# The h of a feed-forward transposed by VectorE and a round trip through device memory

## The chip, the cores and the metric

One core of a Trainium2 chip runs the whole kernel. The metric is the device time of one execution in microseconds (us). The kernel before takes 1023.84 us, the median of three runs (1023.41 to 1024.4). Engines are named as in the profile: PE is TensorE, DVE is VectorE, ACT is ScalarE, POOL is GpSimd, SP is SyncE, whose queue issues nearly all DMAs.

## The reference

Two layers, each a half-step SwiGLU feed-forward, a token mixer of four head groups and a second half-step SwiGLU, then a final RMS norm. There are 256 tokens, 1024 columns, and 2816 columns inside a feed-forward. The change touches the four feed-forwards alone:

```
def swiglu(x, w_gate, w_up, w_down):
    return (jax.nn.silu(x @ w_gate) * (x @ w_up)) @ w_down

for l in range(DEPTH):
    x = x + 0.5 * swiglu(rms_norm(x, norm_ffn1[l]), ffn1_w_gate[l], ffn1_w_up[l], ffn1_w_down[l])
    x = x + hybrid_mixer(rms_norm(x, norm_mix[l]), ...)
    x = x + 0.5 * swiglu(rms_norm(x, norm_ffn2[l]), ffn2_w_gate[l], ffn2_w_up[l], ffn2_w_down[l])
```

All is float32. The kernel gets there by splitting every factor of a product into a rounded high part and a low part and multiplying three times.

## The kernel before, in words

The tokens are two halves, h = 0 and h = 1, of 128 each. The weights come as *sets* of 128 x 1024 numbers (512 KB) in one list for the whole program. Loading a set (`Set.load`) is a DMA into one of four raw buffers, an ACT instruction that rounds it to `whi`, and a DVE instruction that subtracts to `wlo`; there are eight buffers of these. Using a set (`Set.mm`) is six matmuls of 512 columns: for each of two row blocks `hi x whi`, `hi x wlo`, `lo x whi`.

A feed-forward has 11 chunks of 256 inner columns. A chunk is four sets of gate and up columns (s = 0 to 3, `gate_up`), whose product gathers in one PSUM bank `ps_g`; after s = 3, ACT takes the silu and DVE multiplies, which gives `sg`, 128 tokens x 256 columns, the h of the reference. The product with `w_down` wants it the other way round, columns on partitions. So `turn` waits three turns and lets TensorE transpose two blocks of 128 x 128 into PSUM; ACT and DVE split that into `hhi` and `hlo`. After the gate and up sets of chunk c come the two sets of `w_down` of chunk c - 1 (`down_`), summed in `ps_d0` and `ps_d1` over the 11 chunks.

The loop at the end calls `consume(0, i)` for the set i and `consume(1, i - 5)` for the other half, five sets later (two at the very start). Each `consume` loads two sets ahead, issues the six matmuls and then calls `advance`, which counts down the waits of all spawned generators: a "turn" is one `consume`. On this recorded program lies a scheduler, which puts the instructions of each engine in an order of its own, within their dependences; an engine then runs its list strictly in order. SP too: a DMA that waits for its data or its buffer holds up all DMAs behind it.

Of the kernel before, what the change touches and what calls it, by code (L numbers as in the profile page):

```python
# [9 lines left out]
F32 = mybir.dt.float32  # L10
F32R = mybir.dt.float32r
# [4 lines left out]
P = 128  # L16
# [9 lines left out]
AHEAD = 2  # L26
TURN_X = 1
TURN_H = 3
WARM = 30
FIRST = 12  # L30
FIRST_LAG = 2
# [14 lines left out]
)  # L46
WIDTH = dict(SPLITS)
GW = tuple(sum(WIDTH[n] for n in g) for g in GROUPS)
# Rows of w_out in the order in which the heads are done: NSA, FoX, dilated, sinks.
OROWS = (2, 3, 0, 1, 6, 7, 4, 5)  # L50


# [1 line left out]
def hybrid_kernel(ctx: ExitStack, tc: tile.TileContext, a: dict, out: bass.AP):  # L54
    nc = tc.nc
# [5 lines left out]
    hbuf = pool("hbuf", 2)  # L61
    gains = pool("gains", 1)
    work = pool("work", 2)
    small = pool("small", 4)
    ps = pool("ps", 2, space=PSUM)
    dram = pool("dram", 2, space=bass.MemoryType.DRAM)

    def bank(tag):
        return ps.tile([P, 512], F32, name=f"ps_{tag}")
# [20 lines left out]
            for g in tbl:  # L90
                nc.sync.dma_start(tbl[g], a[f"c_{g}"])

    # The array runs at half its clock until it has been busy for a while.
    idle = const.tile([P, P], mybir.dt.bfloat16, name="idle")
    nc.vector.memset(idle, 0.0)
    one = const.tile([P, 1], F32, name="one")
# [8 lines left out]
        return bass.AP(tensor=src.tensor, offset=src.offset, ap=[[0, P], [1, n]])  # L105

    class Set:
        """Two row blocks of a weight by up to 512 of its columns."""

        def __init__(self, src, n, use):  # L110
            self.src, self.n, self.use = src, n, use
# [39 lines left out]
    running = [[], []]  # L151

    def spawn(gen):
        """Runs gen, which yields how many turns it lets pass."""
        wait = next(gen, None)
        if wait is not None:
            alive.append([gen, wait])

    def queue(h, gen):
        """As spawn, one after the other for each h; one that yields 0 lets the next begin."""  # L160
        lines[h].append(gen)

    def advance():
# [21 lines left out]
        begins.setdefault((i, h), []).append(f)  # L185

    class Norm:
        """RMS norm of x: its product with the gain, transposed, in two parts, for the matrix
        products; the scale of each token goes onto what these return."""

        def __init__(self, src, final=False):
            self.src, self.final = src, final
# [2 lines left out]
            self.parts = {}  # L195

        def load(self, before):
            """Fetches the gain, well before the sets from this one on."""
            self.gain = gains.tile([P, D], F32, name="gain")
            with tc.issue_after(sets[before - 8].dma.ins):  # L200
                nc.sync.dma_start(self.gain, bcast(self.src, D))

        def take(self, h, c):
            """Half c of the columns of x[h] is final."""
            if c == 0:
                self.stat[h] = small.tile([P, 2], F32, name="stat")
            sl = slice(c * 512, (c + 1) * 512)
            xg = work.tile([P, 512], F32, name="xn")
            self.first = nc.vector.tensor_tensor(xg, x[h][:, sl], self.gain[:, sl], op=ALU.mult)
            norm_stat(h, c, self.stat[h])  # L210
            if self.final:
                self.xg[h, c] = xg
            else:
                spawn(self.turn(h, c, xg))
            if c == 1:
                self.scale[h] = rstd_of(self.stat[h])

        def take_turned(self, h, c):
            """As take, of the kernel's input, which is there in both layouts."""
            xg = work.tile([P, 512], F32, name="xn").rearrange("p (k t) -> p k t", t=P)  # L220
            nc.sync.dma_start(xg, a["xT"][h, c])
            g = gcol[:, 4 * c:4 * c + 4].unsqueeze(2).to_broadcast([P, 4, P])
            self.first = nc.vector.tensor_tensor(xg, xg, g, op=ALU.mult)
            hi, lo = (big.tile([P, 4, P], F32R, name=f"x{t}{h}{c}") for t in ("hi", "lo"))
            split_T(xg, hi, lo)
            self.parts[h, c] = hi, lo
# [14 lines left out]
            self.parts[h, c] = hi, lo  # L241

        def blocks(self, h, ks):
            """The stationary operands of some blocks of 128 columns."""
            while any((h, k // 4) not in self.parts for k in ks):
                advance()
            return tuple([self.parts[h, k // 4][t][:, k % 4, :] for k in ks] for t in range(2))
# [6 lines left out]
    def add_ffn(norm, gu, down, nxt):  # L254
        phases.append(len(sets))
        hT = {}
        acc = {}

        def turn(h, c, hh):
            yield TURN_H  # L260
            pt = quad("t")
            for j in range(2):
                nc.tensor.transpose(pt[:, j, :], hh[:, j * P:(j + 1) * P], ident)  # L263
            hT[h, c] = tuple(hbuf.tile([P, 2, P], F32R, name=f"h{t}{h}") for t in ("hi", "lo"))
            split_T(pt[:, :2, :], *hT[h, c])

        def gate_up(h, c, s, st):
            if s == 0:
                acc[h] = bank("g")
            st.mm(acc[h], *norm.blocks(h, (2 * s, 2 * s + 1)), s == 0, s == 3)  # L270
            if s == 3:
                sg = work.tile([P, 256], F32, name="sg")
                r = norm.scale[h]
                nc.scalar.activation(sg, acc[h][:, :256], AF.Silu, scale=r)  # L274
                nc.vector.scalar_tensor_tensor(sg, acc[h][:, 256:], r, sg, op0=ALU.mult, op1=ALU.mult)  # L275
                spawn(turn(h, c, sg))

        def down_(h, c, d, st):
            if c == 0:
                acc[h, d] = bank(f"d{h}")  # L280
            hi, lo = hT[h, c]
            st.mm(acc[h, d], [hi[:, k, :] for k in range(2)], [lo[:, k, :] for k in range(2)], c == 0, c == 10)
            if c == 10:
                residual(h, d, acc[h, d], 0.5, nxt)

        def add_down(c):
            for d in range(2):
                sets.append(Set(down[c, d], 512, lambda h, st, d=d: down_(h, c, d, st)))

        for c in range(11):  # L290
            for s in range(4):
                sets.append(Set(gu[c, s], 512, lambda h, st, c=c, s=s: gate_up(h, c, s, st)))
            if c > 0:
                add_down(c - 1)
        add_down(10)

    def add_mixer(l, norm, nxt):
# [28 lines left out]
                V[name] = big.tile([P, 2, n, 64], F32, name=f"v_{name}")  # L326

        def tr(z, n):
            """Transposes n pieces of 128 columns into one bank."""
            pt = quad("t")  # L330
            for j in range(n):
                nc.tensor.transpose(pt[:, j, :], z[:, j * P:(j + 1) * P], ident)  # L332
            return pt

        def dup(dst, src, n, r):
            """n heads of 64 columns, each twice."""
            scaled(dst.rearrange("p (n t d) -> p n t d", n=n, t=2),
                   src.rearrange("p (n d) -> p n d", n=n).unsqueeze(2).to_broadcast([P, n, 2, 64]), r)

# [4 lines left out]
            nc.scalar.activation(dst, src, AF.Copy, scale=r)  # L344

        def scores(qT, keys, nk, tag):
            """Minus q k^T, for even and for odd heads, in a bank each."""
            views = [bank(tag)[:, :2 * nk].rearrange("p (j k) -> p j k", j=2) for _ in range(2)]
            for i in range(4):
                r = slice(64 * (i % 2), 64 * (i % 2) + 64)  # L350
                dst = views[i % 2][:, i // 2, :]
                nc.tensor.matmul(dst, qT[r, i // 2, :], keys(i)[r, :nk], start=True, stop=True)  # L352
            return views

        def softmax(h, views, table, nk, sink=None, guard=False):
            """exp(least - s) of the negated scores, and one over its sums."""
            p = work.tile([P, 4, P * (h + 1)], F32, name=f"p{h}")[:, :, :nk]
            nm = small.tile([P, 4], F32, name="nm")
            den = small.tile([P, 4], F32, name="den")
# [59 lines left out]
            return put  # L419

        def put_part(h, first, last):
            """Adds up the branches of NSA."""
            def put(o):
                if first:
                    M["on", h] = work.tile([P, 2, P], F32, name="on")
                    nc.scalar.activation(M["on", h], o, AF.Copy)
                else:
                    nc.vector.tensor_tensor(M["on", h], o, M["on", h], op=ALU.add)
                if last:
                    hi, lo = oT[h]  # L430
                    split_T(M["on", h], hi[:, 0:2, :], lo[:, 0:2, :])
                    ready[h].add(0)
            return put
# [46 lines left out]
                              lambda i, n: M["vc"], put_part(h, False, True), NB, f"d{h}", gate=0, guard=True)  # L480

        def log_sigmoid(h, z, r):
            """min(z, 0) - log(1 + exp(-|z|)); the logarithm as 2 artanh(e / (2 + e))."""
            sm = lambda n: small.tile([P, 4], F32, name=n, bufs=2)
            zf = sm("zf")
            nc.vector.scalar_tensor_tensor(zf, z, r, M["fb"], op0=ALU.mult, op1=ALU.add)
# [18 lines left out]
            nc.vector.scalar_tensor_tensor(M["lf", h], q, -2.0, m0, op0=ALU.mult, op1=ALU.add)  # L505

        def forget(h):
            """The sums of log f up to each key, to all partitions, with the causal mask on the
            block of the queries themselves."""
            yield 2  # L510
            pc = bank("t")
            if h == 0:
# [231 lines left out]


def _layout(i):
    """The inputs as the kernel reads them: the same numbers, in another order."""
    f = lambda n: np.asarray(i[n], np.float32) if np.asarray(i[n]).dtype != np.float32 else np.asarray(i[n])
    r = {"x": f("x").reshape(2, P, D)}
    r["xT"] = np.ascontiguousarray(r["x"].reshape(2, P, 2, 4, P).transpose(0, 2, 4, 3, 1))  # L750
# [38 lines left out]
```

## Time and profile before

| | |
|---|---|
| median of three runs | 1023.84 us |
| span of the profiled execution, first to last instruction | 1021.8 us |
| its own time | not listed; the timed median is 2.0 us over the span |
| PE busy | 1007.5 us, 99% of the span |
| PE clock | 0.999 of full speed, on average |
| DMA | 183.53 MB, 179 GB/s over the span |
| wraw loads (512 KB), issue to landing | 3.4 us median |

A busy PE says only that some matmul was under way; two overlap. The distance from one start to the next in the timeline is what a matmul costs. The DMA share is the mean over the 16 DMA engines of the time in which they had a packet in hand.

### The profile page before, as it was taken

The numbers are of one execution on the slowest core, as the hardware profiler recorded it, in microseconds if no ns is written. First come the engines' busy times: TensorE is split into PE (matmuls) and PEld (weight loads), VectorE is DVE, ScalarE is ACT, GpSimd is POOL, SyncE is SP. The second block draws the span as 40 slices with busy tenths as digits, with TensorE's granted clock in tenths as the row PEclk, the third lists the DMA queues.
The fourth block names the chain that finished last, engine by engine and source line by source line (L and its number), as shares of the span: only waits on it lengthen the run. The fifth ranks groups of instructions, "written<-read, shape, count | busy, mean of one in ns | idle before, by whom it ended". The sixth has DMA issues, their size and how long they took to land.

```text
span 1021.8 us, 13721 instructions
## 1 busy us (share of the span) xinstructions
PE 1007.5 (99%) x5046; PEld 814.9 (80%) x5046; DVE 617.5 (60%) x1150; ACT 519.9 (51%) x881; POOL 20.0 (2%) x31
## 2 busy tenths in 40 slices
PE   9999999999999999999999999999999999999996
PEld 6888888867778888888888888888678788888885
DVE  6655555786777455555765555558777665555554
ACT  6544444655665444444544444446566554444442
POOL 0000000010000000000000000000100000000000
PEclk9999999999999999999999999999999999999999
DMA  8955556655344455556656555655634445555551
GB/s 304 304 188 187 186 188 205 189 155 161 119 165 146 162 187 186 185 186 209 186 175 192 185 186 186 211 171 178 200 96 149 133 159 188 193 186 186 185 185 41
DMA packets 56722, 183.53 MB, mean 180 GB/s; under 512 B 7232, under 2 KB 14032, under 8 KB 56656
## 3 DMA queue, kind: packets, MB, share of 16 engines
q1 hardware_dynamic: 55920, 181.09, 54.7%
q0 software_dynamic: 448, 1.06, 0.4%
q8 instruction: 39, 0.64, 0.3%
q10 hardware_dynamic: 288, 0.52, 0.1%
q14 instruction: 27, 0.22, 0.1%
HBM read 181.59 MB, written 1.06 MB: 179 GB/s over the span
## 4 chain that ended last, share of the span: by engine, by line
PE 92%; DVE 5%; ACT 2%; issue 1%; DMA 0%; SPq 0%; POOLq 0%; ACTq 0%
PE ps_g L127 55%; PE ps_d L127 28%; PE ps_t L263 2%; PE ps_t L410 2%; DVE wlo L121 1%; PE ps_t L398 1%; PE ps_d L352 1%; PE ps_t L238 1%; PE ps_t L332 1%; ACT p L369 1%; PE ps_t L352 1%; DVE blk L441 1%; DMA xn<-in_xT 0%; DVE x L251 0%; DVE p L390 0%
## 5 line engine op out<-in xcount | busy, mean ns | idle before, releaser
L121 DVE TENSOR_TENSOR wlo<-wraw,whi 128x1024 fp32r<-128x1024 f32 (+2 forms) x328 | 394.6, 1205 | 285.9 <-ACT whi L119 285.1
L119 ACT ACTIVATE whi<-wraw 128x1024 fp32r<-128x1024 f32 (+2 forms) x328 | 342.2, 1044 | 315.6 <-PE ps_g L127 218.8
L127 PE MATMUL ps_g<-whi,xhi 128*128 128x512 f32 (+2 forms) x896 | 351.0, 392 | 0.6 <-ACT whi L119 0.6
L127 PE MATMUL ps_g<-wlo,xhi 128*128 128x512 f32 (+2 forms) x896 | 347.0, 387 | 0.9 <-DVE wlo L121 0.9
L127 PE MATMUL ps_g<-whi,xlo 128*128 128x512 f32 (+2 forms) x896 | 346.9, 387 | 0.0
L127 PEld LDWEIGHTS ps_g<-whi,xhi 128*128 128x128 f32 x896 | 168.8, 188 | 37.2 <-issue 4.7
L127 PEld LDWEIGHTS ps_g<-wlo,xhi 128*128 128x128 f32 x896 | 168.9, 188 | 32.9 <-DVE wlo L121 1.8
L127 PEld LDWEIGHTS ps_g<-whi,xlo 128*128 128x128 f32 x896 | 168.7, 188 | 31.6 <-issue 0.3
L127 PE MATMUL ps_d<-whi,hhi 128*128 128x512 f32 x352 | 144.2, 410 | 0.5 <-ACT hhi L143 0.5
L127 PE MATMUL ps_d<-whi,hlo 128*128 128x512 f32 x352 | 137.9, 393 | 0.0
L127 PE MATMUL ps_d<-wlo,hhi 128*128 128x512 f32 x352 | 137.5, 391 | 0.0
L127 PEld LDWEIGHTS ps_d<-whi,hlo 128*128 128x128 f32 x352 | 66.1, 188 | 14.4 <-DVE hlo L144 0.2
L274 ACT ACTIVATE sg<-ps_g,rstd 128x256 f32<-128x256 f32 x88 | 41.8, 475 | 69.8 <-PE ps_g L127 67.4
L127 PEld LDWEIGHTS ps_d<-whi,hhi 128*128 128x128 f32 x352 | 66.2, 188 | 12.6 <-ACT hhi L143 1.5
L127 PEld LDWEIGHTS ps_d<-wlo,hhi 128*128 128x128 f32 x352 | 66.4, 189 | 11.5
L275 DVE SCALAR_TENSOR_TENSOR sg<-ps_g,rstd,sg 128x256 f32<-128x256 f32 x88 | 42.4, 481 | 43.3 <-ACT sg L274 43.3
L369 ACT ACTIVATE p<-p,nm 128x128 f32<-128x128 f32 (+2 forms) x96 | 40.1, 421 | 23.1 <-DVE nm L361 10.8
L143 ACT ACTIVATE hhi<-ps_t 128x256 fp32r<-128x256 f32 x88 | 33.0, 375 | 27.2 <-PE ps_t L263 27.2
L144 DVE TENSOR_TENSOR hlo<-ps_t,hhi 128x256 fp32r<-128x256 f32 x88 | 33.8, 417 | 8.5 <-ACT hhi L143 8.5
L263 PEld LDWEIGHTS ps_t<-ident,sg 128*128 128x128 f32 x176 | 24.6, 140 | 11.4
L263 PE MATMUL ps_t<-ident,sg 128*128 128x128 f32 x176 | 33.5, 271 | 0.0
L139 POOL TENSOR_TENSOR rstd<-ms,mhalf 128x1 f32<-128x1 f32 x14 | 8.6, 613 | 940.0 <-DVE ms L137 940.0
(146 smaller groups left out, 593.4 us busy)
## 6 DMA issues: line engine op xcount, KB each, us to landing
wraw<-in_gu SPq DMA_DIRECT2D x176, 512.0 KB, 3.4
wraw<-in_down SPq DMA_DIRECT2D x88, 512.0 KB, 3.4
wraw<-in_win SPq DMA_DIRECT2D x24, 512.0 KB, 4.0
wraw<-in_wout SPq DMA_DIRECT2D x16, 512.0 KB, 3.5
wraw<-in_win SPq DMA_DIRECT2D x16, 384.0 KB, 3.5
wraw<-in_w SPq DMA_DIRECT2D x8, 512.0 KB, 3.4
wraw<-in_win SPq DMA_DIRECT2D x8, 400.0 KB, 3.4
gain<-in_norm_ffn SPq DMA_DIRECT2D x3, 512.0 KB, 4.4
```

The lines of the kernel that those rows point to most:

```text
L119: nc.scalar.activation(self.hi, r, AF.Copy)
L121: nc.vector.tensor_tensor(self.lo, r, self.hi.bitcast(F32), op=ALU.subtract)
L127: nc.tensor.matmul(acc, s, w[:, k, :], start=first and k == 0 and i == 0, stop=last and k == 1 and i == 2)
L143: nc.scalar.activation(hi, pt, AF.Copy)
L144: nc.vector.tensor_tensor(lo, pt, hi.bitcast(F32), op=ALU.subtract)
L238: nc.tensor.transpose(pt[:, j, :], xg[:, j * P:(j + 1) * P], ident)
L263: nc.tensor.transpose(pt[:, j, :], hh[:, j * P:(j + 1) * P], ident)
L274: nc.scalar.activation(sg, acc[h][:, :256], AF.Silu, scale=r)
L275: nc.vector.scalar_tensor_tensor(sg, acc[h][:, 256:], r, sg, op0=ALU.mult, op1=ALU.mult)
L352: nc.tensor.matmul(dst, qT[r, i // 2, :], keys(i)[r, :nk], start=True, stop=True)
L369: nc.scalar.activation(p[:, i, :], p[:, i, :], AF.Exp, bias=nm[:, i:i + 1], scale=-1.0, accum_out=den[:, i:i + 1])
L410: nc.tensor.matmul(o[64 * e:64 * e + 64, j, :], vals(2 * j + e, n), pts[n][:w, 2 * j + e, :], start=n == 0, stop=n == len(blocks) - 1)
```

## The change

The new `turn_far` serves chunks 0 to 9; chunk 10 keeps `turn`. As soon as `sg` is there, DVE transposes each of its 32 x 32 blocks within its place (`st`). The block that belongs at block row b, block column a then still stands at row a, column b. Four DMAs, one for each 32 partitions, write `st` to device memory, 32 partitions x 8 pieces of 128 bytes each. Three turns later one DMA reads it back (`back`, 128 partitions x 2 pieces of 512 bytes), with the blocks in their places, and three turns after that ACT and DVE split it. All five DMAs go through SP's queue. `st` uses the mixer's buffers `z` and `back` its buffers `pT`. `down_` calls `advance` until its h is there. The pool in device memory gets four buffers in place of two. The rest of the diff takes comments out.

```
-    dram = pool("dram", 2, space=bass.MemoryType.DRAM)
+    dram = pool("dram", 4, space=bass.MemoryType.DRAM)
...
+FAR = 3
...
+        def turn_far(h, c, hh):
+            st = work.tile([P, 512], F32, name="z")[:, :256]
+            nc.vector.transpose(st, hh)
+            far = dram.tile([8, 32, 4, 32], F32, name="far")
+            for a_ in range(4):
+                nc.sync.dma_start(far[:, :, a_, :].rearrange("b j i -> j b i"),
+                                  st[32 * a_:32 * a_ + 32].rearrange("p (b i) -> p b i", i=32))
+            yield FAR
+            back = work.tile([P, 4, P], F32, name="pT")[:, :2, :]
+            nc.sync.dma_start(back, far.rearrange("(k b) j a i -> (b j) k (a i)", k=2))
+            yield FAR
+            hT[h, c] = tuple(hbuf.tile([P, 2, P], F32R, name=f"h{t}{h}") for t in ("hi", "lo"))
+            split_T(back, *hT[h, c])
...
-                spawn(turn(h, c, sg))
+                spawn((turn if c == 10 else turn_far)(h, c, sg))
...
+            while (h, c) not in hT:
+                advance()
```

SP's queue of one chunk of the first feed-forward, before (numbers tell buffers apart; `in_gu1` are the gate and up sets, `in_down1` the sets of `w_down`):

```order
L116 DMA wraw_1238<-in_down1 128x1024
L116 DMA wraw_1259<-in_down1 128x1024
L116 DMA wraw_1287<-in_gu1 128x1024
L116 DMA wraw_1312<-in_gu1 128x1024
L116 DMA wraw_1331<-in_gu1 128x1024
L116 DMA wraw_1350<-in_gu1 128x1024
```

The same of the kernel after, where line numbers are higher by one; `far_925` belongs to h = 1, `far_947` to h = 0:

```order
L275 DMA far_925<-z_923 32x8x32 x4
L117 DMA wraw_930<-in_down1 128x1024
L117 DMA wraw_960<-in_gu1 128x1024
L275 DMA far_947<-z_945 32x8x32 x4
L279 DMA pT_958<-far_925 128x2x128
L117 DMA wraw_980<-in_gu1 128x1024
L279 DMA pT_972<-far_947 128x2x128
L117 DMA wraw_1007<-in_gu1 128x1024
L117 DMA wraw_1026<-in_gu1 128x1024
L117 DMA wraw_1044<-in_down1 128x1024
```

Of six DMAs to a chunk there are sixteen now, ten rows here: the writes wait for their transpose on DVE and the reads for the landing of their writes, and the loads stand behind them. In the other feed-forwards the writes stand one load sooner or later; the reads stand before the last gate and up loads of the chunk there too.

ACT in one chunk before (`hhi1` and `hhi0` are split from PSUM, where TensorE wrote them):

```order
L274 ACTIVATE sg_996<-ps_g_934,rstd_274 128x256
L119 ACTIVATE whi_1001<-wraw_999 128x1024
L274 ACTIVATE sg_1011<-ps_g_947,rstd_219 128x256
L119 ACTIVATE whi_1029<-wraw_1027 128x1024
L143 ACTIVATE hhi1_1023<-ps_t_1020 128x256
L143 ACTIVATE hhi0_1042<-ps_t_1039 128x256
L119 ACTIVATE whi_1054<-wraw_1052 128x1024
L119 ACTIVATE whi_1073<-wraw_1071 128x1024
```

and after, where they are split from the read-back tile `pT`:

```order
L291 ACTIVATE sg_942<-ps_g_871,rstd_219 128x256
L120 ACTIVATE whi_932<-wraw_930 128x1024
L120 ACTIVATE whi_962<-wraw_960 128x1024
L291 ACTIVATE sg_1062<-ps_g_996,rstd_274 128x256
L144 ACTIVATE hhi1_992<-pT_958 128x256
L120 ACTIVATE whi_982<-wraw_980 128x1024
L144 ACTIVATE hhi0_1003<-pT_972 128x256
L120 ACTIVATE whi_1009<-wraw_1007 128x1024
L120 ACTIVATE whi_1028<-wraw_1026 128x1024
L120 ACTIVATE whi_1046<-wraw_1044 128x1024
L291 ACTIVATE sg_1084<-ps_g_1013,rstd_219 128x256
```

Both splits now wait for a DMA, with the rounding of the next sets behind them. The silu of h = 1 (`sg_1062`) now comes two sets after that of h = 0 of the same chunk (`sg_942`); before, it stood just ahead of that of the next chunk.

PE around the transposes of h = 0 before (`ps_t<-ident,sg`):

```order
L127 MATMUL ps_d0_391<-whi_980,hhi0_912 128x512
L127 MATMUL ps_d0_391<-wlo_981,hhi0_912 128x512
L127 MATMUL ps_d0_391<-whi_980,hlo0_913 128x512
L263 MATMUL ps_t_1039<-ident_86,sg_1011 128x128 x2
L127 MATMUL ps_d1_472<-whi_871,hhi1_893 128x512
L127 MATMUL ps_d1_472<-wlo_872,hhi1_893 128x512
L127 MATMUL ps_d1_472<-whi_871,hlo1_894 128x512
L127 MATMUL ps_d1_472<-whi_871,hhi1_893 128x512
```

and the last matmuls of the gate and up sets of h = 0 in the kernel after (`ps_g_1013` is h = 0, `ps_g_1138` h = 1; buffers 1009 and 1010 are of the set s = 2, 1028 and 1029 of s = 3):

```order
L128 MATMUL ps_g_1013<-wlo_1010,xhi01_181 128x512
L128 MATMUL ps_g_1013<-whi_1009,xlo01_182 128x512
L128 MATMUL ps_g_1013<-whi_1009,xhi01_181 128x512
L128 MATMUL ps_g_1013<-wlo_1010,xhi01_181 128x512
L128 MATMUL ps_g_1013<-whi_1009,xlo01_182 128x512
L128 MATMUL ps_g_1013<-whi_1028,xhi01_181 128x512
L128 MATMUL ps_g_1138<-whi_982,xhi10_224 128x512
L128 MATMUL ps_g_1013<-wlo_1029,xhi01_181 128x512
L128 MATMUL ps_g_1013<-whi_1028,xlo01_182 128x512
L128 MATMUL ps_g_1013<-whi_1028,xhi01_181 128x512
L128 MATMUL ps_g_1013<-wlo_1029,xhi01_181 128x512
L128 MATMUL ps_g_1013<-whi_1028,xlo01_182 128x512
```

The transposes are gone (8 pairs are left in the program, of chunks 10, where there were 88). Single matmuls of h = 1 now stand between those of h = 0 that wait for `whi` and those that wait for `wlo`, and h = 1 uses a set one to three sets after h = 0, not five.

## Rows read from the trace of the kernel before

**Rows 1.** The page, part 1: busy time, share of the span, instructions of each engine.
```profile
PE 1007.5 (99%) x5046; PEld 814.9 (80%) x5046; DVE 617.5 (60%) x1150; ACT 519.9 (51%) x881; POOL 20.0 (2%) x31
```

**Rows 2.** The page, part 4: the chain that ended last, by engine and line.
```profile
PE 92%; DVE 5%; ACT 2%; issue 1%; DMA 0%; SPq 0%; POOLq 0%; ACTq 0%
PE ps_g L127 55%; PE ps_d L127 28%; PE ps_t L263 2%; PE ps_t L410 2%; DVE wlo L121 1%; PE ps_t L398 1%; PE ps_d L352 1%; PE ps_t L238 1%; PE ps_t L332 1%; ACT p L369 1%; PE ps_t L352 1%; DVE blk L441 1%; DMA xn<-in_xT 0%; DVE x L251 0%; DVE p L390 0%
```

**Rows 3.** The chain in order of time, 410 to 440 us: start, duration, what.
```profile
412.93 10.88 PE ps_g L127 x48
423.81 1.36 PE ps_d L127 x6
425.18 0.22 PE ps_t L263 x2
425.39 1.40 PE ps_d L127 x6
```

**Rows 4.** The timeline of SP's queue (start, us, what): two stretches.
```profile
151.97 0.43 SPq L313 DMA_DIRECT2D fb<-in_fox_b_f  x1
152.44 0.42 SPq L314 DMA_DIRECT2D sinkin<-in_swa_sinks  x1
...
410.78 0.33 SPq L116 DMA_DIRECT2D wraw<-in_down  x1
...
427.61 0.33 SPq L116 DMA_DIRECT2D wraw<-in_down  x1
```

**Rows 5.** The timeline of one h product, same columns, with what ended a wait.
```profile
422.06 0.39 PE L127 MATMUL ps_g<-whi,xlo 128*128 128x512 f32 x1
422.49 0.47 ACT L274 ACTIVATE sg<-ps_g,rstd 128x256 f32<-128x256 f32 x1 [1.66 <-PE ps_g L127]
423.00 0.48 DVE L275 SCALAR_TENSOR_TENSOR sg<-ps_g,rstd,sg 128x256 f32<-128x256 f32 x1 [0.91 <-ACT sg L274]
```

**Rows 6.** Busy time in two stretches: length, engines, clock, DMA share, GB/s.
```profile
0.00:50.00 50.00, 47.46 (x211) 37.33 (x212) 31.64 (x42) 29.63 (x43) 1.52 (x7) 1.00 0.87 304
349.00:467.00 118.00, 118.00 (x535) 97.29 (x534) 62.61 (x72) 54.62 (x70) 0.00 (x0) 1.00 0.58 189
```

**Rows 7.** Groups by line and shape: count, busy us, mean ns, idle before.
```profile
L121 DVE TENSOR_TENSOR wlo<-wraw,whi 128x1024 fp32r<-128x1024 f32 x304 | 371.5, 1224 | 277.1 <-ACT whi L119 276.5
L119 ACT ACTIVATE whi<-wraw 128x1024 fp32r<-128x1024 f32 x304 | 321.9, 1060 | 299.2 <-PE ps_g L127 202.6 <-PE ps_d L127 91.4 <-PE ps_t L263 1.5
L403 DVE COPY pT<-ps_t 128x512 f32<-128x512 f32 x10 | 6.9, 688 | 9.8 <-PE ps_t L398 6.6 <-PE ps_t L410 3.2
L390 DVE TENSOR_SCALAR p<-p,rd 128x256 f32<-128x256 f32 x24 | 6.8, 350 | 0.1
```

**Rows 8.** The DMA view: queue share; issues with KB each, median us to landing.
```profile
q1 hardware_dynamic: 55920, 181.09, 54.7%
wraw<-in_gu SPq DMA_DIRECT2D x176, 512.0 KB, 3.4
out_y<-xn SPq DMA_DIRECT2D x2, 256.0 KB, 2.0
line<-ct POOLq DMA_DIRECT2D x4, 2.0 KB, 3.0
gcol<-in_gcol SPq DMA_DIRECT2D x1, 4.0 KB, 1.7
```

**Rows 9.** The DMA view, 657.8 to 658.2 us: small packets and their busy share.
```profile
DMA packets 237, 0.01 MB, mean 36 GB/s; under 512 B 237, under 2 KB 237, under 8 KB 237
q1 hardware_dynamic: 237, 0.01, 38.3%
```

**Rows 10.** Waits of SP's queue: us in total, times, longest.
```profile
SPq L116 <- DVE wlo L121: 590.4, 235, 12.6
```

**Rows 11.** The DMA view, 42 to 46 us, where other loads share the queue.
```profile
wraw<-in_down SPq DMA_DIRECT2D x1, 512.0 KB, 5.7
```

## The prediction

> **What bounds the kernel now.** Read first the busy shares [rows 1]: PE 99%, its weight loads (PEld, which overlap it) 80%, DVE 60%, ACT 51%. That alone proves little, since matmuls overlap, so the chain that ended last comes next [rows 2]: 92% of the span is PE, and 83% is the two groups of matmuls that use the sets, ps_g and ps_d of line 127. The transposes of h (L263) are 2%. Then the chain in order of time [rows 3] gives prices: 48 matmuls take 10.88 us, 0.2267 each, and the feed-forward's stretch is these without a gap. SP's queue shows the same beat: the first w_down load of one chunk is issued at 410.78 and of the next at 427.61 [rows 4], 16.83 us to a chunk. The 72 matmuls of a chunk (6 sets, 2 halves, 6 each) are 72 x 0.2267 = 16.32 of that. The other 0.51 is two transposing turns. In a long stretch of a feed-forward [rows 6] PE is busy 118.00 of 118 us at a granted clock of 1.00, the higher of the two levels, 2.4 GHz; DVE 62.61, ACT 54.62, DMA share 0.58. SP waits mostly for wlo to free a raw buffer [rows 10]: loads are held back, not hurried. So every slot that leaves PE is time, as long as the sets still come in time.
>
> **What is removed.** A pair of transposes is 0.22 us in the chain, and the six matmuls behind it take 1.40 instead of 1.36 [rows 3]: 0.26, which agrees with the 0.51 for two. Of 88 turns 80 go (10 chunks, 2 halves, 4 feed-forwards): 80 x 0.255 = 20.4 us. ACT and DVE still split h, from SBUF instead of PSUM, which I leave at nothing; both have idle time for it.
>
> The Trainium skill prices the step otherwise: its page "VectorE: DVE Perf Modes", section "The three transpose paths", gives TensorE 390 ns for a 128 x 128 transpose (in bf16), and would have 160 x 0.39 = 62 us go. The row shows 0.22 us for two in a full queue, and it decides.
>
> **What is added, off PE.** A turn adds one DVE transpose of 128 x 256. No row shows one. The nearest are a DVE pass over the same shape, 350 ns, and one over twice the columns, 688 [rows 7]; I take 0.35, so 0.7 us to a chunk beside 62.61 / 118 x 16.83 = 8.9 us of DVE now. It is hidden under PE.
>
> It adds four writes and one read on SP. An issue takes 0.47 us from one to the next [rows 4]: ten more to a chunk, sixteen in all, 7.5 of 16.3 us. No bound.
>
> On the DMA engines a turn adds 4 x 256 packets of 128 bytes, 64 for each of 16 engines, and a read of 128 KB. A set costs 0.58 x 118 us / 42 sets = 1.63 us of the engines, so the read 0.41. The writes are the unknown: no row shows 128 bytes going to device memory. Below: 237 packets under 512 bytes, nearly all reads, took 38.3% of 16 engines for 0.4 us [rows 9], 10 ns each. Above: a packet of the page's mean, mostly 4 KB, takes 0.547 x 1021.8 x 16 / 55920 = 160 ns [rows 8]. I take 18 ns, near the lower row, since these packets are small but not as small: 1.15 us to a turn. The DMA work of a chunk is then 9.8 + 2 x (1.15 + 0.41) = 12.9 of 16.3 us. It fits, but not by much.
>
> The Trainium skill speaks against it: "DMA: Bandwidth & Descriptors", section "Specifications", says that transfers under 512 bytes are read, modified and written. From its 27 GiB/s to an engine, 512 bytes read and written would be some 35 ns a packet, an estimate. No run here shows it yet; by it the DMA work of a chunk would be 15.1 us, and the forecast below would stand.
>
> **What is added on the path: SP's order.** SP was free to run ahead; now the loads stand behind writes that wait for a product of the same chunk, and reads that wait for those writes. So there are two loops from one chunk's writes to the next, and each must be shorter than 16.32 us, or it, not PE, sets the beat. I follow the first feed-forward's order as shown with the change.
>
> Common head, from the last gate matmul of h = 0: a matmul's tail beyond its slot and the hop to ACT 0.20, silu to product 0.51, product 0.48 [rows 5], transpose 0.35, hop 0.10: 1.64 us.
>
> Loop A, through the read for h = 1 and the load of set s = 1 behind it: head 1.64, four write issues 1.88, the read's issue 0.47, the load 3.4 to landing [rows 8] plus 0.41 behind the read, whi 1.06 and wlo 1.23 [rows 7] with a hop of 0.05, and then the 22 matmuls from there to the end of s = 3 (the last 12 are in the order shown), 4.99. Sum 15.1: slack 1.2 us.
>
> Loop B, through the read for h = 0, which waits for its writes: head 1.64, three issues 1.41, the fourth write's landing, the read's issue 0.47, the load of s = 2 3.81, whi, wlo and hop 2.34, 12 matmuls 2.72. A DMA lands at least after 1.7 us (gcol, 4 KB); the writes to device memory took 2.0 (out_y) and 3.0 (line) [rows 8]. With 2.0 the sum is 14.4: slack 1.9, so a landing up to 3.9 us costs nothing.
>
> Both are under 16.32, so PE stays the bound: queued behind the waiting reads are three loads, with over a microsecond to spare, and behind the splits on ACT the rounding of the same sets, which would wait for their loads anyway. With packets at p each, the writes delay loop A by 64p - 2.35 us and land 64p + 0.4 after the last issue; either slack is used up near p = 55 ns. From there each microsecond costs 40 (chunks with round trips).
>
> **The start.** In the first 50 us the DMA share is 0.87 [rows 6], with inputs, tables and the first sets in one queue: 6.5 us free. Seven turns fall into it, 7 x 1.56 = 10.9 us: 4.4 too much, of which I take 4.0. At 10 ns it would be 0.9, at 55 ns 21. After the mixers the weights flow already; I add nothing.
>
> **The sum.** Profiled span 1021.8 - 20.4 + 4.0 = 1005.4; with the 2.0 us by which the median stands above the span, 1007.4. Own range: 1002 to 1016 (start from 0.9 to 11 us, transposes' price by 10%).
>
> **Rivals.**
> - *The small writes set the beat* (slower). Place: the read for h = 0 on SP, waiting for the fourth write. It decides from 55 ns a packet. For it: between 10 and 160 ns nothing is shown, and pieces of 128 bytes in steps of 512 are new to this kernel. Against: the small reads at 10 ns. At 75 ns: 64 x 0.020 = 1.3 us x 40 = 51, so 1059. At the far end, 160 ns, the engines would need 9.8 + 0.8 + 20.5 = 31.1 us to a chunk, 14.8 x 40 = 590 more; I give that next to nothing.
> - *The loads land later, behind the others.* Loop A has 1.2 us to spare for the load's 3.4. Where other loads shared the queue one took 5.7 [rows 11]; at that, 2.3 - 1.2 = 1.1 x 40 = 44, so 1051; at 5.0 it would be 0.4 x 40 = 16, so 1023, which is no change. For it: the loads now leave SP in bunches of three. Against: in loop A only a read of 128 KB is ahead.
> - *The transposes cost PE more than the chain shows*, as the skill's 390 ns would have it: 1007 - 42 = 965. The beat of 16.83 speaks against it.
> - *The change does not take the transposes away*: excluded by the order, where 8 pairs of 88 are left.
>
> **How the numbers follow.** Forecast 0.62; small writes 0.18; later loads 0.17, a third of it with no change or a small gain; dearer transposes 0.02; the rest 0.01. Range 1001 to 1050: it leaves out under 0.05 below and some 0.15 above. About 0.2%, 2 us, is what a measurement of this kernel can tell from no change. Faster takes the forecast, the dearer transposes and a little of the late loads: 0.66; same 0.06; slower 0.28.
>
> **What would show it.** Right: a beat of 16.3 us between first w_down loads, PE's chain at 0.227 us a matmul in the feed-forwards, writes landing under 3.9 us, and the time lost mostly before 60 us. Wrong: PE waiting for whi or wlo at s = 1 or s = 2 of every chunk; SP's reads waiting for far for several us; a DMA share near 1 in the feed-forwards; a granted clock of half where PE pauses. If the beat is over 16.8, the forecast is wrong, whatever the reason.

## The result and the profile after

The kernel after takes 1034.33 us (median of four runs, 1033.16 to 1036.79) against 1024.12 of the kernel before beside it: a ratio of 1.0103, interval 1.0087 to 1.0119. It is slower, by 10 us, where a gain of 16 was forecast (1007.4 from 1023.84). Its profiled execution took 1033.17 us, with a span of 1031.4.

The page, parts 1 and 4, answering to [rows 1, 2]:

```profile
PE 1001.0 (97%) x4886; PEld 800.8 (78%) x4886; DVE 649.6 (63%) x1230; ACT 518.9 (50%) x881; POOL 21.4 (2%) x31
...
PE 77%; DMA 7%; DVE 7%; ACT 4%; issue 2%; SPq 2%; POOLq 0%; POOL 0%; ACTq 0%; DVEq 0%
```

PE lost 160 matmuls and 6.5 us of busy time, yet the span grew: PE's share of the chain fell from 92% to 77%, and DMA, SP and ACT have come into it. What they wait for, in the view of the waits (us in total, times, longest), answers to [rows 10]:

```profile
SPq L275 <- DVE z L272: 208.2, 67, 7.9
SPq L117 <- DVE wlo L122: 206.4, 103, 12.6
...
SPq L279 <- DMA far<-z: 18.8, 19, 3.0
```
```profile
ACT whi L120 <- DMA wraw<-in_gu: 99.7, 84, 3.3
ACT hhi L144 <- DMA pT<-far: 61.1, 29, 4.9
```

SP used to wait 590 us for free buffers, which is a reserve. Of that, 206 is left; as much again goes into writes (L275) that wait for VectorE's transpose, with loads standing behind them. Hence ACT waits 84 times for gate and up loads. In the DMA view the median load takes 4.4 or 6.0 us to landing, against 3.4 in [rows 8]; the median write takes 1.7:

```profile
wraw<-in_gu SPq DMA_DIRECT2D x176, 512.0 KB, 4.4
wraw<-in_down SPq DMA_DIRECT2D x88, 512.0 KB, 6.0
far<-z SPq DMA_DIRECT2D x320, 32.0 KB, 1.7
pT<-far SPq DMA_DIRECT2D x80, 128.0 KB, 3.2
```

**Where the time went.** A feed-forward ends with its fourth `x<-ps_d` on DVE. From the end of the stage ahead of it to there, the four took 199.7, 188.6, 188.5 and 186.9 us before and 209.1, 187.6, 190.6 and 185.4 after; the mixers changed by under half a microsecond. So the first lost 9.4 us, the third 2.1, and the second and fourth won 1.0 and 1.5, where 5 were expected of each.

Three places show it. The first is the start. SP's timeline at 60 to 80 us (start, us, what):

```profile
60.29 4.07 SPq L275 DMA_DIRECT2D far<-z  x8
64.53 0.38 SPq L279 DMA_DIRECT2D pT<-far  x1
64.96 0.47 SPq L117 DMA_DIRECT2D wraw<-in_gu  x1
...
68.33 0.84 SPq L92 DMA_DIRECT2D tbl_cmp<-in_c_cmp  x1
69.34 0.54 SPq L279 DMA_DIRECT2D pT<-far  x1
69.92 2.55 SPq L117 DMA_DIRECT2D wraw<-in_gu  x3
```

and what the chain makes of it, followed by PE in two windows (length, then busy time and count of PE, PEld, DVE, ACT, POOL, the clock, the DMA share, GB/s):

```profile
69.92 6.87 DMA wraw<-in_gu
...
76.87 1.06 ACT whi L120
...
77.96 1.23 DVE wlo L122
```
```profile
70.00:80.00 10.00, 8.08 (x34) 5.84 (x33) 4.54 (x6) 4.52 (x6) 0.00 (x0) 1.00 0.99 358
...
189.00:195.00 6.00, 3.73 (x9) 2.63 (x9) 5.18 (x7) 4.38 (x6) 0.00 (x0) 0.72 0.35 115
```

Between the issue of one gate load at 64.96 and of the next at 69.92 stand seven table loads and a read; then three loads go out together, and the one that PE needs lands 6.87 us later. The first window holds 34 matmuls where ten microseconds hold 44 at 0.227.

The second place is the beat of the first feed-forward. The first of four writes of h = 0 leaves SP at these times, 16.7 and 16.8 us apart, hardly shorter than the 16.83 of [rows 4]:

```profile
119.53 1.81 SPq L275 DMA_DIRECT2D far<-z  x4
...
136.19 1.80 SPq L275 DMA_DIRECT2D far<-z  x4
138.10 0.40 SPq L279 DMA_DIRECT2D pT<-far  x1
138.54 0.47 SPq L117 DMA_DIRECT2D wraw<-in_gu  x1
139.29 0.37 SPq L279 DMA_DIRECT2D pT<-far  x1
139.77 0.87 SPq L117 DMA_DIRECT2D wraw<-in_gu  x2
...
152.96 1.81 SPq L275 DMA_DIRECT2D far<-z  x4
```

The chain there is loop B, term by term:

```profile
139.77 6.18 DMA wraw<-in_gu
...
146.03 1.07 ACT whi L120
...
147.13 1.24 DVE wlo L122
...
148.41 3.01 PE ps_g L128 x12
```

First write to issue of the read 3.10 (139.29 - 136.19), to the load 0.48, landing 6.18, rounding and subtraction 2.46, twelve matmuls 3.01, head 1.54 (152.96 - 151.42): 16.77 us.

The third is the end of the first and of the third feed-forward: the window 189 to 195 us above has nine matmuls in six microseconds, at a clock of 0.72. It is not the landing of a load that PE waits for there. SP issues two loads of `w_down` at 180.65, and the first of them lands 5.0 us after its issue, at 185.6 (SP's timeline, and the DMA view at 180.6 to 180.7 us):

```profile
180.65 0.96 SPq L117 DMA_DIRECT2D wraw<-in_down  x2
```
```profile
wraw<-in_down SPq DMA_DIRECT2D x1, 512.0 KB, 5.0
```

ACT rounds it only at 189.61, because in ACT's list its rounding stands behind a split and the last silu of h = 1, which both wait for PE. The chain there:

```profile
188.50 0.71 PE ps_g L128 x3
...
189.24 0.02 ACT sg L291
...
189.61 1.05 ACT whi L120
...
190.69 1.24 DVE wlo L122
...
191.97 8.23 PE ps_d L128 x29
```

PE waits first for the rounding and then for the subtraction: three starts of matmuls, at 188.80, 190.71 and 191.97, take 2.7 us more than two slots of 0.227. Behind that the clock is at its lower level (0.50 at 192 to 194 us, in the last view below), and the matmuls up to 195 us lose some 1.5 us more. The third feed-forward ends in the same way at 693 to 700 us; the second and the fourth have neither this pause nor the lower clock.

### The profile page after: what moved, and what is told of

It reads as the page before. It is cut to its first block, busy times and chain, and to the rows that moved or that the text cites. A ratio compares the mean times of both kernels' runs of the same rounds, so it can differ in the third digit from the quotient of the medians.

```text
span 1031.4 us, 14151 instructions
## 1 busy us (share of the span) xinstructions
PE 1001.0 (97%) x4886; PEld 800.8 (78%) x4886; DVE 649.6 (63%) x1230; ACT 518.9 (50%) x881; POOL 21.4 (2%) x31
## 3 DMA queue, kind: packets, MB, share of 16 engines
q1 hardware_dynamic: 164720, 202.09, 62.9%
## 4 chain that ended last, share of the span: by engine, by line
PE 77%; DMA 7%; DVE 7%; ACT 4%; issue 2%; SPq 2%; POOLq 0%; POOL 0%; ACTq 0%; DVEq 0%
PE ps_g L128 47%; PE ps_d L128 23%; DMA wraw<-in_gu 5%; DVE wlo L122 2%; ACT whi L120 2%; PE ps_t L429 2%; SPq L275 1%; PE ps_t L417 1%; PE ps_d L371 1%; DMA pT<-far 1%; ACT p L388 1%; PE ps_t L239 1%; PE ps_t L351 1%; DMA wraw<-in_down 1%; PE ps_t L371 1%
## 5 line engine op out<-in xcount | busy, mean ns | idle before, releaser
L128 PE MATMUL ps_g<-whi,xhi 128*128 128x512 f32 (+2 forms) x896 | 346.6, 394 | 5.0 <-ACT whi L120 3.3
L128 PE MATMUL ps_d<-whi,hhi 128*128 128x512 f32 x352 | 138.4, 397 | 5.3 <-ACT whi L120 3.0
L144 ACT ACTIVATE hhi<-pT 128x256 fp32r<-128x256 f32 x80 | 32.7, 409 | 61.2 <-DMA pT<-far 61.1
L145 DVE TENSOR_TENSOR hlo<-pT,hhi 128x256 fp32r<-128x256 f32 x80 | 33.6, 420 | 39.0 <-ACT hhi L144 39.0
L272 DVE STREAM_TRANSPOSE z<-sg 128x256 f32<-128x256 f32 x80 | 35.5, 444 | 2.1
L128 PE MATMUL ps_d<-whi,ohi 128*128 128x512 f32 x64 | 26.1, 408 | 0.0
```

Source lines behind the costliest of these rows:

```text
L128: nc.tensor.matmul(acc, s, w[:, k, :], start=first and k == 0 and i == 0, stop=last and k == 1 and i == 2)
L144: nc.scalar.activation(hi, pt, AF.Copy)
L145: nc.vector.tensor_tensor(lo, pt, hi.bitcast(F32), op=ALU.subtract)
L272: nc.vector.transpose(st, hh)
```

## The experiments

Theory: what PE gained is real; SP's one list, in which loads now stand behind writes and reads that wait, makes them late and takes it back. Rivals: the small packets and the extra bytes load the DMA engines; the slots on PE are worth less; h itself comes too late. Each ratio is to the kernel before, run beside it on the same chip.

| run | h's trip | us | ratio, interval | the four feed-forwards, us |
|---|---|---|---|---|
| before | none, TensorE | 1024.1 to 1024.5 | 1 | 199.7, 188.6, 188.5, 186.9 |
| after | SP | 1034.3 | 1.0103, 1.0087 to 1.0119 | 209.1, 187.6, 190.6, 185.4 |
| e1 | left out | 1004.0 | 0.9803, 0.9789 to 0.9818 | 196.2, 183.6, 183.4, 181.9 |
| e2 | POOL | 1038.7 | 1.0148, 1.0119 to 1.0177 | 210.5, 190.7, 191.4, 184.4 |
| e3 | SP, not in the first | 1025.4 | 1.0006, 0.9996 to 1.0015 | 201.2, 187.6, 190.8, 186.1 |
| e4 | SP, unused | 1035.5 | 1.0106, 1.0089 to 1.0124 | 212.0, 189.7, 186.1, 187.1 |
| e5 | POOL, unused | 1024.9 | 1.0001, 0.9991 to 1.0011 | 202.6, 188.7, 188.5, 187.0 |
| e6 | SP, w_down later | 1035.6 | 1.0107, 1.0087 to 1.0127 | 206.7, 188.4, 191.2, 186.1 |
| e9 | POOL, long time | 1009.8 | 0.9862, 0.9848 to 0.9877 | 196.7, 183.6, 183.8, 182.5 |
| e11 | write SP, read POOL | 1028.0 | 1.0041, 1.0026 to 1.0056 | 214.5, 184.1, 185.4, 182.4 |
| e12 | SP, long time | 1035.9 | 1.0108, 1.0091 to 1.0125 | 208.6, 189.2, 187.1, 185.6 |

**e1: the transposes' worth.** The writes and the read go, and the split reads `st`:

```
-            far = dram.tile([8, 32, 4, 32], F32, name="far")
...
-            nc.sync.dma_start(back, far.rearrange("(k b) j a i -> (b j) k (a i)", k=2))
-            yield FAR
+            yield TURN_H
...
-            split_T(back, *hT[h, c])
+            split_T(st.rearrange("p (k t) -> p k t", t=P), *hT[h, c])
```

> Keeps VectorE's block transpose but leaves out the round trip: the splits read the transposed blocks straight from SBUF, so the blocks are not exchanged and the output is not the reference's. SP has loads alone. Theory (SP's order costs the time; the removed transposes are worth 20.4 us): 1024 - 20 = 1004 us, within 3. Rival (the slots that leave PE are worth less, since VectorE's 444 ns transposes and the changed order of the matmuls take some back): 1012 us or more.

It took 1004.0 us, 20.5 less, and the beat is 16.3 from end to end. So the removed term was right, VectorE's transposes are hidden, and all of the loss is in the round trip.

This run also shows where the loss lies. Both traces have 4886 instructions on PE, so the n-th of them can be set beside the n-th. The kernel after is 4.7 us behind e1 at 84 us, 7.1 at 188 (the beats of the first feed-forward, 2.4), 13.3 at 230 (its end and the first of the mixer, 6.2), 13.1 at 335, 15.5 at 530 (the second feed-forward, 2.4), 18.5 at 692, 24.7 at 735 (the end of the third, with the first of the mixer, 6.2), 24.6 at 840 and 27.8 at the end. So each of the two ends costs more than the start, and far more than the beats; the second feed-forward gives back only 2.4 of its 5 us.

**e4 and e5: the trip beside the old way.** TensorE's `turn` makes h; `turn_far` runs too, without its split. In e5 the five DMAs are POOL's.

```
-                spawn((turn if c == 10 else turn_far)(h, c, sg))
+                spawn(turn(h, c, sg))
+                if c < 10:
+                    spawn(turn_far(h, c, sg))
...
-                nc.sync.dma_start(far[...], ...)      # e5 alone
+                nc.gpsimd.dma_start(far[...], ...)
```

> TensorE's transposes make h as before, and the round trip is done beside them with its result unused. PE's work is that of before. Theory (loads wait in SP's list behind writes and reads, whoever uses them): 1024 plus what the order costs, 1035 to 1054 us. Rival (only the wait of h for its own read costs): 1024 to 1028 us.

> As the run with the unused round trip (TensorE makes h), but POOL issues the trip, so that SP has loads alone, in the order of before; bytes and transfers are the same. That run lost 12.3 us in the first feed-forward and nothing in the other three. Theory (SP's list: loads behind writes that wait): the loss goes, under 1027 us, and the first feed-forward ends before 202 us. Rival (the DMA engines, which are nearly full in the first 50 us, have 1.8 MB more to move there): it stays, 1032 to 1038 us.

From SP the unused trip costs 11 us, all of it in the first feed-forward (12.3 by the profiled executions); from POOL the same bytes cost nothing measurable, though the first feed-forward of its profiled execution ended at 202.6 us, just over the 202 expected. Of these 12.3, 2.3 are not the trip's, nor are 2.7 of the 2.9 that e5's lost: they arise by 16 us, behind an input (`xn`) that landed at 7.6 and 8.3 us instead of 6.3, and the first write of a trip is issued after 21 us. With SP, ACT waited 34.0 us for gate and up loads; with POOL, 7.7:

```profile
ACT whi L120 <- DMA wraw<-in_gu: 34.0, 27, 6.0
```
```profile
ACT whi L120 <- DMA wraw<-in_gu: 7.7, 9, 2.3
```

So what the first feed-forward loses, at its start and at its end, comes with the trip in SP's list and not from the DMA engines. In the later three, at the old beat of 16.8, SP's list costs nothing even so.

**e3: the start alone.** `spawn` takes `turn` in the first feed-forward.

> The first feed-forward keeps TensorE's transposes; the other three have the round trip. Theory (the first feed-forward lost 9.4 us where 5.1 were to be won, 14 of it by its start, where the DMA queue is full): its end comes back from 208.4 to 199.0 us, the rest stays as after, 1034.3 - 9.4 = 1025 us, within 3. Rival (a loss of the steady beat that every feed-forward shares, so that nothing hangs on the start): the later ones show beats over 16.8 and the sum stays over 1030.

As the theory had it: 1025.4, the first feed-forward back at 201.2, and the later ones as after to within 0.7. The change therefore loses 9 us in the first and wins nothing, on balance, in the other three.

**e2: another queue alone.** All five DMAs of the trip on `nc.gpsimd`, nothing else.

> The whole change, with its five DMAs to a turn issued by POOL, so that SP has loads alone, in the order of before. Theory (loads held behind waiting writes and reads in SP's list): most of the 30 us comes back, 1004 to 1012 us, and ACT's wait for gate and up loads falls from 100 us to under 30. Rival (the DMA engines are the limit: 1024 small packets and 256 KB to a turn cost the same from any queue): 1028 to 1036 us, as after. A third way, POOL's issues too slow for ten in a chunk: a beat over 17 us and more than 1040.

It took 1038.7 us, so the theory's forecast failed, though the half on the loads held: ACT's wait for gate and up loads is 1.9 us. Another wait has come in its place, and the chain shows it (pieces in order of time):

```profile
ACT hhi L144 <- DMA pT<-far: 197.3, 73, 8.6
```
```profile
401.44 4.05 POOL far L275 x7
405.49 3.90 DMA far<-z
...
410.04 5.85 DMA pT<-far
...
415.92 0.04 ACT hhi L144
...
416.24 1.05 ACT whi L120
```

Issues on POOL take 0.58 us for a write, and the eight writes of both halves go out together; the last of them lands 3.9 us after its issue, and the second half's read 5.9 after its own. The split of h stands on ACT four roundings after its silu, some 11 us; the trips of both take 14.5 (401.44 to 415.89), and further roundings stand behind the split. The time lies between those of the rival on the DMA engines and of the third way, and e5 and e9, which move the same bytes from POOL, speak against both.

**e6, e7, e8: more time for h, on SP.** The two w_down sets of a chunk go two sets later in the list:

```
             for s in range(4):
                 sets.append(Set(gu[c, s], ...))
-            if c > 0:
-                add_down(c - 1)
-        add_down(10)
+                if s == 1 and c > 1:
+                    add_down(c - 2)
+        add_down(9)
+        add_down(10)
```

> The whole change, with the two w_down sets of a chunk used two sets later than after (between the gate and up sets 1 and 2 of the chunk after the next), so that h has 5.4 us more for its round trip. Theory (in the later feed-forwards the loop from one chunk's product through SP's writes and reads to the loads behind them decides, and h is needed too early): beats of 16.3 us there, 4 x 3 us won on after: 1018 to 1024 us; the start still costs its 12. Rival (it is not h's wait but the loads behind the reads that are late; these stand as before in SP's list): no change on after, 1030 to 1036.

> As the run with w_down two sets later; besides, the read is recorded five turns behind the writes and the split four behind the read (three and three after), and the first four chunks of the first feed-forward keep TensorE's transposes. Theory: the start's 12 us go as well, PE is the bound again: 1024 - 76 x 0.255 = 1005, with 2 to 5 us for the ends of the feed-forwards 1005 to 1010 us. Rival (late loads behind the reads): 1018 or more.

> A control: TensorE's transposes in all chunks, no round trip, w_down two sets later. Both theories: 1022 to 1026 us, since PE's work is that of before and only its order changes. If it is below 1020, the later w_down brings a gain of its own.

e6 took 1035.6 us and did nothing, which speaks for the rival that its expectation names: the loads are late, wherever h is used. e7 took 1027.6 us (1.0034, 1.0024 to 1.0043), also the rival's; with TensorE at the start it wins that back, and no more. The control e8 took 1026.9 (1.0023, 1.0014 to 1.0032), a little slower than before and just over the range expected, so the later w_down brings nothing of its own.

**e11: only the reads leave SP.** `back` is read by `nc.gpsimd`.

> As after, but POOL issues the read; the writes stay on SP. Theory (loop B: a load behind the read for h = 0 and landing 6.2 us after its issue because of what is ahead of it): without the reads in SP's list the later feed-forwards come to 16.3 us a chunk and the first one's start is half as dear: 1012 to 1022 us. Rival (h comes too late for its split, whoever issues; POOL's read adds about a microsecond): 1034 to 1042 us.

Neither time was met, and the stages tell why. The later three run at 184.1, 185.4 and 182.4 us, a beat of 16.3: with the reads out of SP's list, and the order that follows from that, the gain is there. The first is worse than after, 214.5. Its chain at 104 to 137 us runs from the writes through the read for h = 0, which lands 5.9 to 6.1 us after its issue on POOL with four loads just ahead of it, and through the split to the rounding behind it. The beat there is 16.7 to 16.9: it is now h that comes too late.

**e9 and e12: both edits, and one taken back.** POOL issues the trip, w_down as in e6, six turns to the read and seven to the split, and the split is ordered behind the rounding of the latest loaded set:

```
-            nc.scalar.activation(self.hi, r, AF.Copy)
+            self.round = nc.scalar.activation(self.hi, r, AF.Copy)
...
-            split_T(back, *hT[h, c])
+            with tc.issue_after(sets[done[0] - 1].round.ins):
+                split_T(back, *hT[h, c])
```

> POOL issues the round trip, the w_down sets of a chunk are used two sets later, the read is recorded six turns behind the writes, and the splits stand on ACT and DVE behind the rounding of the latest loaded set, six roundings after the silu of their chunk where there were four. Theory (both waits gone: SP has loads alone, and h has 16 us where POOL's trip takes 13 to 14): PE is the bound again, 1003 to 1010 us, beats of 16.3 in all feed-forwards, ACT's wait for pT under 40 us against 197 in the run with POOL's queue alone. Rival (bytes and small packets slow the loads themselves): beats over 16.8 and 1020 us or more.

> The kernel of the run that came to 1009.8 us, with one thing changed back: SP issues the round trip, so the loads stand behind its writes and reads again, while h has its 16 us. It completes a square: SP or POOL, short or long time for h (1034.3 short on SP, 1038.7 short on POOL, 1009.8 long on POOL). Theory (the loads in SP's list and the time for h are two causes, and neither edit does alone): 1020 us or more, with late loads in the first feed-forward. Rival (the time for h is the whole cause, and POOL's queue only shows it): 1005 to 1014 us.

e9 took 1009.8 us, 1.4% less than before and 2.4% less than after (0.9862 / 1.0103). PE is the bound again: of the chain 88% is PE, ACT waits 9.7 us for h, and a stretch of a feed-forward reads

```profile
398.01 10.98 PE ps_g L128 x48
408.99 5.44 PE ps_d L128 x24
414.43 10.95 PE ps_g L128 x48
```
```profile
ACT hhi L144 <- DMA pT<-far: 9.7, 6, 3.4
...
ACT whi L120 <- DMA wraw<-in_gu: 3.8, 8, 0.8
```

that is, 16.4 us a chunk. With the same time for h but SP as the issuer it is 1035.9, and loads are late again:

```profile
ACT whi L120 <- DMA wraw<-in_gu: 87.4, 53, 5.1
```

The square is complete: SP and short 1034, POOL and short 1039, SP and long 1036, POOL and long 1010. Either cause alone is enough to lose the gain; both have to go. e9 and e12 differ in the issuer alone; the longer time for h is three edits together, which no run takes apart.

**e10: ACT as the issuer**, else as e9, with five turns and five.

> The same with ACT as the issuing engine (writes behind the second silu, reads one and two roundings later; five and five turns). Theory: SP's list is free; ACT pays for ten issues to a chunk and for waits of a microsecond or two in its list, which its idle half can bear: 1003 to 1012 us. Rival (a list in which loads' roundings stand behind waiting DMAs is as bad on ACT as on SP): 1022 us or more.

It took 1019.6 us (0.9953, 0.9939 to 0.9968), between the two times expected, and between SP's 1035.9 and POOL's 1009.8. Since its turns are shorter as well, it does not show what ACT's list alone costs.

## Why the prediction was wrong, step by step

- *Removed, 20.4 us*: right; e1 measured 20.5.
- *VectorE's transpose, 0.35 us, hidden*: it took 0.444, and was hidden (e1).
- *Packets at 18 ns; the small writes a rival*: the queue's share rose from 54.7% of 1021.8 us [rows 8] to 62.9% of 1031.4, which is 89.8 us x 16 engines over 108800 packets more: 13 ns. The median write landed in 1.7 us, under the 2.0 taken. The rival is refuted; e5 and e9 move the same bytes without loss.
- *Loop B, 14.4 us, slack 1.9*: **this is the step that failed**, with the conclusion drawn from it, and in it one term, the load of s = 2 at 3.81 us. It measured 6.18, and 5.8 to 6.1 in the neighbouring chunks; 14.4 - 3.81 + 6.18 = 16.8, the beat of the first feed-forward. The working put a read of 128 KB ahead of that load, but not the load of s = 1, issued 1.2 us earlier and itself under way, nor the second read. [Rows 11] had a nearer price, 5.7 us where other loads share the queue, at which the sum would have been 16.3 and no slack left. That rival got 0.17; its cause was right and its place, loop A, was not.
- *Both under 16.32, so PE stays the bound*: this fails with it. But the beats explain 2.4 us of the 28 by which the kernel after stands behind e1. Apart from the start, 4.7, the rest lies where the sum had nothing: 6.2 us each at the ends of the first and the third feed-forward, 2.4 in the second, 3.0 in the third before its end and 3.2 in the fourth. Forty equal chunks were the wrong sum. On balance the later three won nothing (e3); e11 has the reads off SP's list, and there the second and fourth run at 16.3 us a chunk and the later three end after 184.1, 185.4 and 182.4 us.
- *The start, 4.0 us, from DMA work*: the size was nearly right (2.0 us behind e1 by 60 us, 4.7 by 84), the mechanism wrong. The same DMA work from POOL costs nothing measurable (e5, ratio 1.0001); from SP it is late loads. The sum left out that the seven table loads and the first reads stand in the same list. That the size came out is luck.
- *Splits behind waiting reads: the roundings behind them "would wait for their loads anyway"*: so it is in loop B, where the rounding follows the landing at once (146.03 after 145.95), but not at the end of the first feed-forward, where the load had landed 4.0 us before its rounding, which stood behind a split from PSUM and the silu in ACT's list. On POOL (e2) ACT's wait for h, with roundings behind it, is the largest that took the place of the late loads, 197 us.

The Trainium skill, "Trainium Kernel Development and Optimization", section "Key Constraints", says that issuing from several engines only saves the sequencer's issue time, since all queues share the same DMA engines. Taken alone, that would make e9 and e12 equal. They are 26 us apart: here the second queue also takes the waits off the loads.

The third feed-forward came out slower than the second mainly by its end: 2.7 us of PE waiting for a rounding and a subtraction and some 1.7 of the lower clock, which the second does not have. That ACT's order does this is read from the trace; no run changes that order alone. Open is also why the scheduler puts the rounding there in the kernel after, and which of the three edits for h's time e9 needs.

## What to carry over

A DMA that waits, put into a queue that carries the loads, is priced by what stands behind it: take the landing time of a load that leaves in a bunch, not the median of loads that leave alone. Give such a trip a queue of its own, and count the whole trip (issues, two landings) against the place where its consumer stands in an in-order engine. Moving one of the two can show nothing, since either is enough to lose the gain. And price the ends of a stage as well as its beat: there a rounding late in ACT's list and the lower clock behind it cost more than the longer beat did.

## What the runs showed of the hardware

- The granted clock fell to its lower level, 1.2 GHz, behind PE's pauses at the end of the first feed-forward, and matmuls then stood 0.43 us apart. PE alone in windows of 2 us (busy, count, clock, DMA share, GB/s):

```profile
188.00:190.00 2.00, 1.20 (x7) 1.00 0.72 207
190.00:192.00 2.00, 0.54 (x2) 0.87 0.01 5
192.00:194.00 2.00, 2.00 (x5) 0.50 0.28 78
194.00:196.00 2.00, 2.00 (x9) 0.78 0.86 252
196.00:198.00 2.00, 2.00 (x11) 1.00 0.98 278
```

PE's pause at 76 to 79 us, at the start, left the clock at 1.00 (the window 70 to 80 us above).
- From POOL the trip is 176 packets a turn (14528 - 448 over 80), from SP 1360; the engines' time for it is nearly the same, 1.0 (8.5% of 1006.8 us in e9, less 0.3%) and 1.1 us a turn.
- On POOL an issue took 0.59 us for a write and 0.72 for a read, on average (e9); on SP it was 0.47 from one to the next.
